# A sixth leading projection, earlier first weights and split norm steps in a two-layer diffusion trunk

## The chip, the cores and the metric

The kernel runs on one core of one Trainium2 chip. The core has five engines that work side by side: PE (matrix products; its weight loads are shown as PEld), DVE (vector operations), ACT (activations and copies), POOL (a slower general engine that here issues stores and computes powers) and SP (which here only issues loads). 16 DMA engines move data between the chip's main memory and the core. The metric is the time of one execution in microseconds (us). The time before is the median of 3 runs.

## The reference

A trunk of two layers handles two groups of tokens that share weights: 128 context tokens and 512 latent tokens, each a row of 2048 values in float32. Per layer:

```python
hp = rms_norm(xp, norm_g[layer]) * (1.0 + sc_p) + sh_p
hs = rms_norm(xs, norm_g[layer]) * (1.0 + sc_s) + sh_s
...
qa, ka, va, ga, ub, bb, cb, gb = split_cols(h @ w_in, EVEN_SPLIT)
...
y_a = merge_heads(o) * jax.nn.silu(ga)
y_b = gated_short_conv(ub, bb, cb, conv_w) * jax.nn.silu(gb)
return jnp.concatenate([y_a, y_b], axis=-1) @ w_out, new
```

Shift, scale and gate (`sh`, `sc`, `gt`) come from a conditioning product `silu(cond) @ ada_w + ada_b`, a weight matrix of 2048 x 6144 per layer with only two rows of input (one for the context tokens, one for the latent ones). `h @ w_in` is the input projection: in layer 0, 6656 columns for attention with a window (queries, keys, values, gate) and for a short gated convolution (u, b, c and its gate). Layer 1 has 6656 columns for two other kinds of attention. An output projection of 2048 x 2048 and a gated residual end each layer. The outputs are the new tokens and the keys and values of the context tokens.

## The kernel before, in words

**Layout.** Activations lie transposed: 128 features on the partitions, 640 tokens along a row (512 latent, then 128 context), so that a projection tile is 128 output columns x 640 tokens. Each of its two halves of 320 tokens is a PSUM buffer (`pa`, `pb`, or a half of `Sp`). Full float32 precision is had from three products of a high and a low part: `wh*hi`, `wh*lo`, `wl*hi` (lines 244 to 246). The inner dimension of 2048 is 16 chunks of 128, handled in four **quarters** of four chunks. The weights of a tile and quarter (256 KB) are loaded by SP (`load_raw`, line 225) into one of four `raw` buffers and split by ACT and DVE (`split`, lines 212 and 213) into four `wh` and four `wl` buffers.

**The leading stretch of layer 0.** `x_block` transposes and squares the input tokens. `ada_on_pe` (line 148) computes 512 columns of the conditioning product: it loads 2 MB pieces into two buffers by turns (line 155), multiplies them on PE (line 158, `T<-ada,sT`), copies (161), transposes (164) and adds up. Blocks 4 and 0 (scale and shift of the first four chunks) are computed first. Then `run_tiles` (line 277) takes the tiles of the input projection, called jobs. Its first few jobs **lead**: quarter after quarter, the normed rows `h` of that quarter are made (`h0_maker`, line 732), the conditioning blocks of the next quarter are loaded and multiplied (`ahead`, which is `ada_group`, line 715), and all leading jobs are multiplied by the quarter. The fourth quarter is cut in two. Some leading jobs are named in `TRANS`: they have no PSUM buffer of their own, but share buffer 0, are copied out after each quarter by ACT in the first (line 308) and added by DVE in the later ones (line 310), into a `sum` tile in a pool named `lead`. The others keep a PSUM buffer. Before, five jobs lead: u, k, v, q0 and q1 (the convolution's u, and keys, values and two query heads of the first pair of heads), and u, q0 and q1 are summed outside PSUM.

Of a quarter's leading weights, the first four are loaded before the rows are made, the others between the matmuls (line 302).

**After the lead.** Each later job is multiplied quarter by quarter. Between quarters a `slot` (line 269) advances the generators in `prep` (norms of queries and keys, lines 403 to 512), one step of `attn` (attention of a pair of heads, line 577), and `fill0`, which computes the remaining conditioning blocks on DVE (line 184). The leading jobs' own preparation is begun one by one there (`pending`). A gate job ends in `late_gate_job` (784): SiLU of the gate, then one multiplication of the finished attention output (line 799). `pair_then` (765) gets an empty dictionary in layer 0, so its outputs are copied (775); in layer 1 gates come first (`gate_job`, 1052), and the outputs are multiplied as they come (773). Small tiles named `stg` are in two buffers: a job's staged projection (`stage`, 379), the query norm's two tiles (451, 452) and the gate's (396, 793).

**End of a layer.** The last output tile is multiplied half by half (lines 354 to 370): the first half's four quarters, then `last(pp, 0)`, then the second half's, then `last(pp, 1)`. In layer 0, `out_last` (901) sums squares over the finished layer, takes the power -0.5 on POOL (919) and spreads it over the partitions by small matmuls (914, 922). In layer 1 `fin_last` (1113) adds the residual, transposes and stores.

The order in which an engine meets its instructions is fixed when the kernel is built: a planner goes by the order written and by a model of when operands and buffers are ready, and may put later matmuls ahead of earlier ones that wait. On the chip each engine then goes through its list in that order.

Of the kernel before, what the change touches and what calls it, by code (L numbers as in the profile page):

```python
# [11 lines left out]
F32 = mybir.dt.float32  # L12
# [8 lines left out]
P = 128  # L21
# [18 lines left out]

P_BUFS = 4
W_BUFS = 4
TRANS = [0, 3, 4]
GRACE = 3
RAW_AHEAD = 5
SPLIT_AHEAD = 3
# [8 lines left out]
def trunk_kernel(ctx: ExitStack, tc: tile.TileContext, I: dict, O: dict):  # L55
# [33 lines left out]
    vec = const.tile([P, 160], F32, name="vec")  # L89
    open_pool("start")  # L90
    sp = pre = pools["cur"]
    rows_a = pre.tile([P, P], F32, name="rows_a")
    nc.sync.dma_start(rows_a[0:16, :], I["c"].rearrange("b (k p) -> (b k) p", p=P))
    nc.scalar.dma_start(rows_a[16:32, :], I["c_ctx"].rearrange("(k p) -> k p", p=P))
    nc.scalar.dma_start(ident, I["k_ident"])
    nc.scalar.dma_start(rows_a[32:64, :], I["norm_g"].rearrange("l (k p) -> (l k) p", p=P))
    nc.scalar.dma_start(rows_a[64:112, :], I["ada_b"][0].rearrange("(k p) -> k p", p=P))
    rows_b = pre.tile([P, P], F32, name="rows_b")
    nc.scalar.dma_start(rows_b[0:48, :], I["ada_b"][1].rearrange("(k p) -> k p", p=P))
    nc.scalar.dma_start(rows_b[48:72, :], I["b_conv"][0].rearrange("t (k p) -> (t k) p", p=P))  # L100
    nc.scalar.dma_start(rows_b[72:74, :], I["c_out_norm"].rearrange("b (k p) -> (b k) p", p=P))
# [4 lines left out]
    ada_sb = pre.tile([P, 512], F32, name="ada_sb")  # L106
    h_t = [pre.tile([P, NT], F32, name=f"ht{i}") for i in range(2)]

    th = pre.tile([32, P], F32, name="th")
    A.activation(th, rows_a[0:32, :], AF.Tanh, scale=0.5)  # L110
    V.scalar_tensor_tensor(out=rows_a[0:32, :], in0=th, scalar=1.0, in1=rows_a[0:32, :],
                           op0=ALU.add, op1=ALU.mult)
# [116 lines left out]
    def split_w(raw):  # L229
        wh = wpool.tile(raw.shape, F32R, tag="wh", name="wh")  # L230
        wl = wpool.tile(raw.shape, F32R, tag="wl", name="wl")
        split(wh, wl, raw)
        return wh, wl
# [41 lines left out]
            credit[0] -= 1.0  # L275

    def run_tiles(jobs, w_ap, make_h, fill=None, rate=0.0, ahead=None, order=(0, 1, 2, 3), before=None,
                  last=None, by_half=False, trans=[], grace=0, cut=None):
        if trans:
            lp = tc.tile_pool(name="lead", bufs=1, side="right")  # L280
            lead_pool = lp.__enter__()
            sums = {n: lead_pool.tile([P, NT], F32, name=f"sum{n}") for n in trans}
            held = [n for n in range(2 + len(trans)) if n not in trans]

            leads = [n for m in range(len(held) + 1) for n in trans[m:m + 1] + held[m:m + 1]]
            leads += trans[len(held) + 1:]
        else:
            leads, held, lp = list(range(min(3, len(jobs)))), [], None
        lead = len(leads)
        pps = {n: (sums[n][:, 0:HALF], sums[n][:, HALF:NT]) if n in trans  # L290
               else new_pp(1 + held.index(n) if trans else n) for n in leads}
        units = [(pos, qd, js) for pos, qd in enumerate(order) for js in (cut if cut and pos == 3 else [(0, 4)])]
        for ui, (pos, qd, js) in enumerate(units):
            parts = {n: split_w(load_raw(w_ap, jobs[n][0], qd, js)) for n in leads[:W_BUFS]}
            for hv in [HV[:1], HV[1:]] if by_half and pos == 0 else [HV]:
                for k in range(4 * qd + js[0], 4 * qd + js[1]):
                    make_h(k, hv) if by_half else make_h(k)
                if ahead and ui + 1 < len(units):
                    ahead(*units[ui + 1][1:])
                for n in leads:  # L300
                    if n not in parts:
                        parts[n] = split_w(load_raw(w_ap, jobs[n][0], qd, js))
                    if n in trans:
                        pp = new_pp(0)
                        proj_q(pp, parts[n], qd, pos, alone=True, js=js)
                        for i, sl in HV:
                            if ui == 0:
                                A.copy(pps[n][i], pp[i][:, 0:HALF])
                            else:
                                V.tensor_add(pps[n][i], pps[n][i], pp[i][:, 0:HALF])  # L310
                    else:
                        proj_q(pps[n], parts[n], qd, pos, hv, js=js)
                    advance(attn, 1)

        quarters = [(col, qd) for col, _ in jobs[lead:] for qd in range(4)]
        raws, parts = {}, {}

        def run_ahead(t):
            for i in range(len(raws), min(t + RAW_AHEAD, len(quarters))):
                raws[i] = load_raw(w_ap, *quarters[i])  # L320
                j = len(parts)
                if j < t + SPLIT_AHEAD and j <= i:
                    parts[j] = split_w(raws[j])
            for j in range(len(parts), min(t + SPLIT_AHEAD, len(quarters))):
                parts[j] = split_w(raws[j])

        def begin(fn, pp):
            g = fn(pp)
            if g is not None:
                prep.append(g)  # L330
                advance(prep, 1)

        def settle():

            while pending:
                n = pending.pop(0)
                drain(prep)
                if before:
                    before(n)
                begin(jobs[n][1], pps[n])  # L340
            drain(prep)

        pending = list(range(lead))
        run_ahead(0)
        t = 0
        if before:
            settle()
        else:
            n = pending.pop(0)
            begin(jobs[n][1], pps[n])  # L350
        for i in range(lead, len(jobs)):
            fn = jobs[i][1]
            pp = new_pp((i - lead) % 2)
            split_last = last is not None and i == len(jobs) - 1
            for qd in range(4):
                proj_q(pp, parts[t], qd, qd, HV[:1] if split_last else HV)
                if before and qd == 0:
                    before(i)
                t += 1
                run_ahead(t)  # L360
                if pending and not prep:
                    n = pending.pop(0)
                    begin(jobs[n][1], pps[n])
                slot(fill, rate)
            if split_last:
                last(pp, 0)
                for qd in range(4):
                    proj_q(pp, parts[t - 4 + qd], qd, qd, HV[1:])
                last(pp, 1)
                return  # L370
            drain(prep)
            if i >= lead + grace and pending:
                settle()
            if lp and not pending and not prep:
                lp.__exit__(None, None, None)
                lp = None
            begin(fn, pp)
# [349 lines left out]
    ada_on_pe(0, 4)  # L727
    x_rows((0, 1, 2, 3))
    x_rows((4,))
    ada_on_pe(0, 0)  # L730

    def h0_maker(k):
        x = xT[k // 4][:, k % 4, :]
# [23 lines left out]
    def q_job(tag, gain, then=None):  # L757
        return lambda pp: q_gen(pools["cur"], pp, tag, gains[gain], then)

    def y_pair(i):  # L760
        t = pools["cur"].tile([P, 2, NT], F32, tag="y", name="y", bufs=2)
        y[i], y[i + 1] = t[:, 0, :], t[:, 1, :]
        return t

    def pair_then(width, kk, i, banded, gated):

# [74 lines left out]
    for i in range(4):  # L841
        kv, h = i // 2, 2 * i
        if i % 2 == 0:
            jobs.append((EV["k"] + kv * P, k_job("k0", I["cache_a_k"][0, 0, kv], "a_k_norm", O["new_a_k"][0, 0, kv])))
            jobs.append((EV["v"] + kv * P, v_job(I["cache_a_v"][0, 0, kv], O["new_a_v"][0, 0, kv])))
        jobs.append((EV["q"] + h * P, q_job("q0", "a_q_norm")))
        jobs.append((EV["q"] + (h + 1) * P, q_job("q1", "a_q_norm", pair_then(640, "k0", h, True, {}))))
        b_tiles(i)
        for j in (h, h + 1):
            jobs.append((EV["g"] + j * P, late_gate_job(j)))  # L850
    for i in range(4, 8):
        b_tiles(i)
    jobs.insert(0, jobs.pop(4))
    run_tiles(jobs, I["ev_w_in"][0], h0_maker, fill0, FILL0, ada_group, trans=TRANS, grace=GRACE, cut=((0, 2), (2, 4)))
    drain(prep)
    for _ in fill0:
        pass
# [43 lines left out]
    def out_last(pp, h):  # L901
        n, mp, sl = KT - 1, pools["cur"], HV[h][1]
        out_sum(n, pp, CS[:1] if h == 0 else CS[1:])
        if h == 0:
            st["sq"] = mp.tile([P, NT], F32, tag="sq", name="sq", bufs=1)
            st["rbc"] = mp.tile([P, NT], F32, name="rbc")
        A.activation(st["sq"][:, sl], x1[n][:, sl], AF.Square)
        starts = [HALF * h, HALF * h + P, HALF * (h + 1) - P]
        tot = psT()
        ss = small.tile([P, 3], F32, tag="ss", name="ss1")  # L910
        r = small.tile([P, 3], F32, tag="r", name="r1")
        for i, s in enumerate((st["acc"], st["sq"])):
# [4 lines left out]
            else:  # L917
                V.scalar_tensor_tensor(out=ss, in0=tot[:, 4:7], scalar=1.0 / D, in1=ss, op0=ALU.mult, op1=ALU.add)
        G.tensor_tensor(r, ss, half[:, 0:3], op=ALU.pow)
        rt = psT()  # L920
        for b, (o, w) in enumerate(((0, P), (P, P), (2 * P, HALF - 2 * P))):
            PE.matmul(rt[:, o:o + w], r[:, b:b + 1].to_broadcast([P, P]), ident[:, P - w:P], start=True, stop=True)
# [28 lines left out]
    def odd_start():  # L951
# [13 lines left out]
        st["con"] = con  # L965
        nc.sync.dma_start(con, I["c_out_norm"][0].partition_broadcast(P))
        V.tensor_scalar(con, con, 1.0 - LAM_INIT, None, ALU.mult)

    gated = {}

    def diff_then(h):
        def then():
# [76 lines left out]
                yield  # L1049
        save_y(2 * h, 2 * h + 1)  # L1050

    def gate_job(i):
        def f(pp):
            if i % 2 == 0:
                gated[i] = y_pair(i)
            gate(pools["cur"], pp, y[i])
        return f

    jobs = []
    heads = (3, 0, 1, 2)  # L1060
    for n, h in enumerate(heads):
# [51 lines left out]
    def fin_last(pp, h):  # L1113
# [3 lines left out]
            st["ot"] = fp.tile([P, 5, P], F32, tag="rp", name="ot", bufs=3)  # L1117
        xr, ot = st["xr", n], st["ot"]
        fin_sum(n, pp, CS[:1] if h == 0 else CS[1:])
        t = psT()  # L1120
        bs = (0, 1) if h == 0 else (2, 3, 4)
        for i, b in enumerate(bs):
# [59 lines left out]
```

## Time and profile before

| what | before |
|---|---|
| median of 3 runs | 2369.32 us (2366.55 to 2371.73) |
| the profiled execution | 2370.14 us |
| its span, first to last instruction | 2368.4 us |
| PE busy | 2320.9 us, 98% |
| DVE busy | 1368.7 us, 58% |
| ACT busy | 882.1 us, 37% |
| POOL busy | 126.2 us, 5% |
| moved by DMA | 304.08 MB, mean 128 GB/s |

How to read it: the span is cut into 40 equal slices of 59.2 us, and a digit is the busy share of an engine in a slice, in tenths (9 is 90% or more). A busy PE is not PE at its peak, since matmuls overlap; the distance between their starts tells the rate. "L158" is line 158 of the kernel. "a<-b" names what an instruction writes and reads. In a timeline row stand start, duration, engine, line, operation, and in brackets the idle time of the engine just before it with what ended that. SPq is the queue of loads that SP issues. The granted clock is the share of full speed that PE's throttle allowed.

### The profile page before, as it was taken

The numbers are of one execution on the slowest core, as the hardware profiler recorded it, in microseconds if no ns is written. First come the engines' busy times: TensorE is split into PE (matmuls) and PEld (weight loads), VectorE is DVE, ScalarE is ACT, GpSimd is POOL, SyncE is SP. The second block draws the span as 40 slices with busy tenths as digits, with TensorE's granted clock in tenths as the row PEclk, the third lists the DMA queues.
The fourth block names the chain that finished last, engine by engine and source line by source line (L and its number), as shares of the span: only waits on it lengthen the run. The fifth ranks groups of instructions, "written<-read, shape, count | busy, mean of one in ns | idle before, by whom it ended". The sixth has DMA issues, their size and how long they took to land.

```text
span 2368.4 us, 40878 instructions
## 1 busy us (share of the span) xinstructions
PE 2320.9 (98%) x16188; PEld 2246.1 (95%) x16188; DVE 1368.7 (58%) x2700; ACT 882.1 (37%) x1855; POOL 126.2 (5%) x173
## 2 busy tenths in 40 slices
PE   5989999999999999999999999999999999999999
PEld 3779999999999999999999999999999999999999
DVE  3468766765864555667865445354455554576662
ACT  4435442433422223222463443444334444453221
POOL 0000000000000000000010100001000000000000
PEclk8999999999999999999999999999999999999999
DMA  9983415424444445666431222212222212236552
GB/s 325 362 262 107 145 54 160 141 81 133 143 147 121 129 133 180 196 192 196 124 96 56 82 73 69 72 54 85 65 72 59 66 55 72 72 116 215 178 173 78
DMA packets 370045, 304.08 MB, mean 128 GB/s; under 512 B 16721, under 2 KB 310158, under 8 KB 369342
## 3 DMA queue, kind: packets, MB, share of 16 engines
q1 hardware_dynamic: 362448, 273.78, 38.1%
q0 software_dynamic: 6864, 27.47, 3.1%
q8 instruction: 127, 2.08, 0.4%
q14 instruction: 64, 0.52, 0.1%
q10 hardware_dynamic: 542, 0.22, 0.0%
HBM read 273.62 MB, written 27.79 MB: 127 GB/s over the span
## 4 chain that ended last, share of the span: by engine, by line
PE 91%; DMA 4%; DVE 2%; ACT 1%; issue 1%; POOL 0%; SPq 0%; ACTq 0%; DVEq 0%; POOLq 0%
PE pa L244 13%; PE pb L244 12%; PE pb L245 12%; PE pb L246 12%; PE pa L246 12%; PE pa L245 12%; PE T L538 2%; DMA ada<-in_ada_w 2%; PE S L550 1%; PE S L552 1%; PE S L551 1%; PE T L389 1%; PE T L599 1%; PE T L158 1%; DMA raw<-in_ev_w_in 1%
## 5 line engine op out<-in xcount | busy, mean ns | idle before, releaser
L212 ACT ACTIVATE wh<-raw 128x512 fp32r<-128x512 f32 (+1 forms) x549 | 343.6, 627 | 1045.4 <-PE pb L245 919.9
L213 DVE TENSOR_TENSOR wl<-raw,wh 128x512 fp32r<-128x512 f32 (+1 forms) x549 | 375.3, 684 | 556.3 <-ACT wh L212 506.4
L244 PE MATMUL pa<-h,wh 128*128 128x320 f32 x2112 | 669.7, 318 | 6.9 <-ACT h L212 4.9
L244 PE MATMUL pb<-h,wh 128*128 128x320 f32 x2112 | 654.6, 310 | 0.0
L245 PE MATMUL pa<-h,wh 128*128 128x320 f32 x2112 | 654.3, 310 | 0.0
L246 PE MATMUL pb<-h,wl 128*128 128x320 f32 x2112 | 654.1, 310 | 0.0
L246 PE MATMUL pa<-h,wl 128*128 128x320 f32 x2112 | 653.8, 310 | 0.0
L245 PE MATMUL pb<-h,wh 128*128 128x320 f32 x2112 | 653.8, 310 | 0.0
L244 PEld LDWEIGHTS pa<-h,wh 128*128 128x128 f32 x2112 | 397.2, 188 | 25.8 <-issue 16.5
L245 PEld LDWEIGHTS pa<-h,wh 128*128 128x128 f32 x2112 | 397.6, 188 | 3.2 <-issue 1.7
L246 PEld LDWEIGHTS pa<-h,wl 128*128 128x128 f32 x2112 | 396.9, 188 | 2.4 <-issue 2.4
L246 PEld LDWEIGHTS pb<-h,wl 128*128 128x128 f32 x2112 | 397.3, 188 | 1.3 <-issue 1.3
L244 PEld LDWEIGHTS pb<-h,wh 128*128 128x128 f32 x2112 | 397.6, 188 | 0.8 <-issue 0.8
L245 PEld LDWEIGHTS pb<-h,wh 128*128 128x128 f32 x2112 | 397.6, 188 | 0.0
L184 DVE SCALAR_TENSOR_TENSOR acc<-adaw,sT,acc 128x512 f32<-128x512 f32 x480 | 336.5, 746 | 22.9 <-DMA adaw<-in_ada_w 22.4
L524 ACT ACTIVATE p<-S,nm,rq 128x768 f32<-128x768 f32 (+3 forms) x120 | 101.3, 844 | 116.8 <-DVE nm L519 80.6
L517 DVE TENSOR_REDUCE nm<-S 128x1 f32<-128x768 f32 (+3 forms) x120 | 91.9, 766 | 23.3 <-PE S L552 22.8
L212 ACT ACTIVATE pth<-T 128x512 fp32r<-128x512 f32 (+1 forms) x132 | 65.8, 533 | 65.2 <-PE T L538 65.1
L213 DVE TENSOR_TENSOR ptl<-T,pth 128x512 fp32r<-128x512 f32 (+1 forms) x132 | 77.3, 608 | 6.4 <-ACT pth L212 5.1
L538 PE MATMUL T<-ident,p 128*128 128x128 f32 x452 | 64.4, 273 | 0.0
L458 ACT COPY qsw<-qx 32x512 f32<-32x512 f32 x96 | 59.3, 618 | 5.6 <-DVE m L434 4.2
L661 POOL DMA_DIRECT2D yd<-y x32 | 18.0, 561 | 752.3 <-DVE y L799 520.2
(248 smaller groups left out, 2300.1 us busy)
## 6 DMA issues: line engine op xcount, KB each, us to landing
adaw<-in_ada_w SPq DMA_DIRECT2D x256, 256.0 KB, 3.0
raw<-in_od_w_in SPq DMA_DIRECT2D x208, 256.0 KB, 2.8
raw<-in_ev_w_in SPq DMA_DIRECT2D x203, 256.0 KB, 2.9
ada<-in_ada_w SPq DMA_DIRECT2D x16, 2048.0 KB, 10.7
raw<-in_ev_w_out SPq DMA_DIRECT2D x64, 256.0 KB, 3.4
raw<-in_od_w_out SPq DMA_DIRECT2D x64, 256.0 KB, 2.8
yd<-y POOLq DMA_DIRECT2D x32, 320.0 KB, 3.0
yin<-yd SPq DMA_DIRECT2D x28, 320.0 KB, 4.8
```

Source lines behind the costliest of these rows:

```text
L158: PE.matmul(acc[32 * g:32 * g + 32, 0:wd], sT[:, kt, :], w[:, kt % m, :], start=(kt < 4), stop=(kt >= KT - 4), tile_position=(0, 32 * g))
L184: V.scalar_tensor_tensor(out=acc[c], in0=w, scalar=sT[:, kt, c:c + 1], in1=acc[c], op0=ALU.mult, op1=ALU.add)
L212: A.activation(hi, x, AF.Copy)
L213: V.tensor_sub(lo, x, hi)
L244: PE.matmul(ps, wh[:, i, :], hi[:, sl], start=(j == js[0] if alone else (pos == 0 and j == 0)), stop=False)
L245: PE.matmul(ps, wh[:, i, :], lo[:, sl], start=False, stop=False)
L246: PE.matmul(ps, wl[:, i, :], hi[:, sl], start=False, stop=(j == js[1] - 1 if alone else (pos == 3 and j == 3)))
L389: PE.transpose(t[:, i * P:(i + 1) * P], src(b), ident)
L458: A.copy(sw[32 * d:32 * d + 32, :], x[32 * (d ^ 1):32 * (d ^ 1) + 32, 0:NS])
L517: V.tensor_reduce(nm, s, axis=AX.X, op=ALU.max, negate=True)
L524: A.activation(p[:, 0:n], s, AF.Exp, scale=rsc, bias=nm, accum_out=l)
L538: PE.transpose(t[:, i * P:(i + 1) * P], p, ident)
```

## The change

- `TRANS` names a sixth leading job, and the order of the first ten jobs becomes u, k, v, g0, q0, q1, g1, c, b, h (before: u, k, v, q0, q1, c, b, h, g0, g1): the first head's gate leads, the second one's follows first. Six jobs lead, with four `sum` tiles.
- For the first pair of heads the gates are now handled by `gate_job`, and the attention's outputs are multiplied by the gate as they come.
- `ada_on_pe(0, 0)` is called by `run_tiles` (`lead_in`) after the first four weights have been loaded and split, and not before them.
- `out_last` and `fin_last` become generators. Their first part runs after the first half's quarters, and their later steps stand between the quarters of the second half. The last call, for the second half, runs without a break as before.
- The small start tiles `rows_a`, `rows_b` and `th` lie in the weight buffers `raw`, and the scratch memory for POOL's transfers is halved, to 8192 bytes a partition.

```diff
-TRANS = [0, 3, 4]
+TRANS = [0, 3, 4, 5]
...
-    rows_a = pre.tile([P, P], F32, name="rows_a")
+    rows_a = wpool.tile([P, P], F32, tag="raw", name="rows_a")
...
             parts = {n: split_w(load_raw(w_ap, jobs[n][0], qd, js)) for n in leads[:W_BUFS]}
+            if ui == 0 and lead_in:
+                lead_in()
...
             if split_last:
-                last(pp, 0)
+                first = last(pp, 0)
+                next(first)
                 for qd in range(4):
                     proj_q(pp, parts[t - 4 + qd], qd, qd, HV[1:])
-                last(pp, 1)
+                    next(first, None)
+                for _ in last(pp, 1):
+                    pass
                 return
...
-    ada_on_pe(0, 0)
...
+    def gate_job(i):
+        def f(pp):
+            if i - i % 2 not in gated:
+                gated[i - i % 2] = y_pair(i - i % 2)
+            gate(pools["cur"], pp, y[i])
+        return f
...
-        jobs.append((EV["q"] + (h + 1) * P, q_job("q1", "a_q_norm", pair_then(640, "k0", h, True, {}))))
+        jobs.append((EV["q"] + (h + 1) * P, q_job("q1", "a_q_norm", pair_then(640, "k0", h, True, gated))))
         b_tiles(i)
         for j in (h, h + 1):
-            jobs.append((EV["g"] + j * P, late_gate_job(j)))
+            jobs.append((EV["g"] + j * P, late_gate_job(j) if i else gate_job(j)))
...
-    jobs.insert(0, jobs.pop(4))
-    run_tiles(jobs, I["ev_w_in"][0], h0_maker, fill0, FILL0, ada_group, trans=TRANS, grace=GRACE, cut=((0, 2), (2, 4)))
+    u0, c0, b0, h0, g0, g1 = jobs[4:10]
+    jobs[0:10] = [u0, jobs[0], jobs[1], g0, jobs[2], jobs[3], g1, c0, b0, h0]
+    run_tiles(jobs, I["ev_w_in"][0], h0_maker, fill0, FILL0, ada_group, trans=TRANS, grace=GRACE, cut=((0, 2), (2, 4)),
+              lead_in=lambda: ada_on_pe(0, 0))
...
         A.activation(st["sq"][:, sl], x1[n][:, sl], AF.Square)
+        yield
...
         G.tensor_tensor(r, ss, half[:, 0:3], op=ALU.pow)
+        yield
         rt = psT()
...
         fin_sum(n, pp, CS[:1] if h == 0 else CS[1:])
+        yield
         t = psT()
...
-    nc = _bacc.Bacc("TRN2", target_bir_lowering=False, num_devices=1)
+    nc = _bacc.Bacc("TRN2", target_bir_lowering=False, num_devices=1, dynamic_dma_scratch_size=8192)
```

More of the change, by code (lines that the diff above doesn't have):

```diff
@@ L97, in trunk_kernel @@
     nc.scalar.dma_start(rows_a[64:112, :], I["ada_b"][0].rearrange("(k p) -> k p", p=P))
-    rows_b = pre.tile([P, P], F32, name="rows_b")
+    rows_b = wpool.tile([P, P], F32, tag="raw", name="rows_b")
     nc.scalar.dma_start(rows_b[0:48, :], I["ada_b"][1].rearrange("(k p) -> k p", p=P))
@@ L107, in trunk_kernel @@
     h_t = [pre.tile([P, NT], F32, name=f"ht{i}") for i in range(2)]
-    th = pre.tile([32, P], F32, name="th")
+    th = wpool.tile([32, P], F32, tag="raw", name="th")
     A.activation(th, rows_a[0:32, :], AF.Tanh, scale=0.5)
@@ L277, in run_tiles @@
     def run_tiles(jobs, w_ap, make_h, fill=None, rate=0.0, ahead=None, order=(0, 1, 2, 3), before=None,
-                  last=None, by_half=False, trans=[], grace=0, cut=None):
+                  last=None, by_half=False, trans=[], grace=0, cut=None, lead_in=None):
         if trans:
@@ L763, in y_pair @@
         return t
+    gated = {}
+    def gate_job(i):
[4 more added lines that the diff above has]
+        return f
     def pair_then(width, kk, i, banded, gated):
@@ L967, in odd_start @@
         V.tensor_scalar(con, con, 1.0 - LAM_INIT, None, ALU.mult)
-    gated = {}
     def diff_then(h):
@@ L1050, in diff_gen @@
         save_y(2 * h, 2 * h + 1)
[L1052 to L1057, printed above, removed]
+    gated.clear()
     jobs = []
```

## The prediction

> **What bounds the kernel now.** I read the page first, for the busy engine over the whole span, and then short windows of the start, where the page's slices show the only hole.
>
> ```profile
> span 2368.4 us, 40878 instructions
> ...
> PE   5989999999999999999999999999999999999999
> ...
> DMA  9983415424444445666431222212222212236552
> ...
> PE 91%; DMA 4%; DVE 2%; ACT 1%; issue 1%; POOL 0%; SPq 0%; ACTq 0%; DVEq 0%; POOLq 0%
> ```
>
> PE is full in every slice but the first three (180 us), and those are the slices in which the DMA engines are full. So an edit can pay in two ways only: it lets PE do useful work in the opening stretch, where PE sometimes waits for transfers, or it removes a later stall of PE. The profiled execution took 2370.14 us, 1.7 more than its span and 0.8 more than the median of 2369.32; I sum against this span.
>
> The windows view gives, per stretch, busy time and (count) for PE, PEld, DVE, ACT and POOL, then granted clock, DMA share and GB/s.
>
> ```profile
> 40.00:80.00 40.00, 33.38 (x224) 21.87 (x217) 15.05 (x31) 15.80 (x29) 0.00 (x0) 0.91 0.98 347
> 80.00:120.00 40.00, 37.81 (x281) 28.99 (x280) 22.22 (x47) 17.89 (x34) 1.25 (x2) 1.00 1.03 361
> ...
> 51.00:164.00 113.00, 104.06 (x763) 82.42 (x763) 55.17 (x125) 44.55 (x88) 2.31 (x4) 0.96 0.94 323
> 164.00:204.00 40.00, 38.06 (x267) 36.38 (x268) 37.82 (x75) 21.26 (x52) 6.46 (x5) 1.00 0.51 150
> 930.00:1010.00 80.00, 80.00 (x548) 80.00 (x547) 48.30 (x80) 20.82 (x32) 3.12 (x6) 1.00 0.65 205
> ```
>
> From 930 to 1010 almost nothing but projection matmuls runs: 80 us / 548 = **0.146 us** each at full clock. One projection tile is 16 chunks x 3 products x 2 halves = 96 of them, 14.0 us; a quarter of it is 24, 3.5 us. The leading stretch runs from 51 to 164 us: the first row below is its start, the second the first matmul after it, behind the last sum of a leading tile. In it DMA is 94% busy at 323 GB/s (361 while saturated) and PE 104 of 113 us: **both are nearly full**. That is why the sixth leading tile can't be free.
>
> ```profile
> 50.97 0.63 PE L244 MATMUL pa<-h,wh 128*128 128x320 f32 x1 [2.77 <-ACT h L212]
> ...
> 164.63 0.41 PE L244 MATMUL pa<-h,wh 128*128 128x320 f32 x1 [0.75 <-DVE sum L310]
> ```
>
> The waits view of PE for 50 to 164 us (total, times, longest), and the two matmul groups around the longest wait:
>
> ```profile
> PE T L158 <- DMA ada<-in_ada_w: 6.6, 2, 5.1
> PE pa L244 <- ACT h L212: 4.9, 3, 2.8
> ```
> ```profile
> 134.47 1.93 PE L158 MATMUL T<-ada,sT 128*32 128x256 f32 x32
> ...
> 142.67 3.56 PE L158 MATMUL T<-ada,sT 128*32 128x256 f32 x32 [5.12 <-DMA ada<-in_ada_w]
> ```
>
> The last conditioning transfer makes PE idle 5.1 us, and the same 32 matmuls then take 3.56 instead of 1.93 us: 1.6 us more, on a clock that has fallen. Another 1.5 us of transfer wait and 4.9 - 2.8 = 2.1 us of waits for the normed rows remain inside the stretch; the 2.8 stands before its start.
>
> **The change part by part.**
>
> *The sixth leading tile.* It takes 96 matmuls, 14.0 us, from after the stretch into it: -14.0 behind, +14.0 inside, less what fills idle time. When does PE reach the last conditioning matmuls? Three quarters with one more tile put 3 x 3.5 = 10.5 us in front of it, the later start (next edit) 1.5, and of the 3.6 us of smaller waits I take half as filled: 10.5 + 1.5 - 1.8 = 10.2. PE had been ready at 142.67 - 5.12 = 137.55, so now at 147.8. When does the transfer land? Up to there three and a half quarters of 256 KB more are loaded, 0.92 MB, at 361 GB/s 2.5 us: 145.2. So the 5.1 us wait and its 1.6 us of slow clock go, and what is late next is PE itself. Shift of the stretch's end: 14.0 + 1.5 - 1.8 - 6.7 = **+7.0**, against 14.0 us less behind it: **-7.0**. Bounds: if nothing is filled, 14.0 + 1.5 is paid and the edit costs 1.5; if only transfers bind, the last one lands 2.5 later and half a quarter of the sixth tile, 1.8, follows it, which gives +4.3 and -9.7.
>
> The tile's other work stands beside PE. Its sums cost ACT two copies in the first quarter and DVE two additions of 0.48 us in each later piece; its weight splits move from later.
>
> ```profile
> L310 DVE TENSOR_TENSOR sum<-sum,pa x12: 480/486/489, 89.7 to 164.1; 128x320 f32<-128x320 f32 x12
> ```
> ```profile
> 152.80:156.35 3.55, 3.55 (x27) 3.52 (x25) 2.56 (x10) 1.00 (x3) 0.00 (x0) 1.00 0.68 194
> ```
>
> DVE is busy 55 of the 113 us, so there is room. The last two leading tiles now share PSUM buffer 0 back to back; the second row is a place where two such tiles already adjoin (the end of one unit, the start of the next), and PE has no hole there. I take nothing.
>
> *First weights ahead of the second conditioning block.* SP's queue, and who waited on what it brought:
>
> ```profile
> 11.89 23.87 SPq L155 DMA_DIRECT2D ada<-in_ada_w  x4
> 35.81 5.65 SPq L225 DMA_DIRECT2D raw<-in_ev_w_in  x4
> 41.83 22.35 SPq L155 DMA_DIRECT2D ada<-in_ada_w  x4
> ```
> ```profile
> 43.53 1.92 PE L158 MATMUL T<-ada,sT 128*32 128x512 f32 x16 [1.78 <-DMA ada<-in_ada_w]
> 47.54 0.66 PE L164 MATMUL T<-ident,ada_sb 128*128 128x128 f32 x4 [2.08 <-ACT ada_sb L161]
> ```
> ```profile
> 44.16 2.85 ACT L212 ACTIVATE wh<-raw 128x512 fp32r<-128x512 f32 x4 [4.52 <-DMA raw<-in_ev_w_in]
> 46.92 0.57 ACT L161 COPY ada_sb<-T 128x512 f32<-128x512 f32 x1
> ```
>
> Gained: the four splits (2.85 us of ACT) no longer stand between the block's matmuls (done at 45.45) and its copy (46.92), 1.4 us. Lost: the DMA engines are full (0.98 from 40 us on), so 1 MB of weights put in front delays the block's last transfer by 1.05 MB / 361 GB/s = 2.9 us. Net **+1.5** on the first projection matmul (already in the sum above). [...]
>
> *The gate in the attention.* The first pair's five outputs are multiplied by the gate on DVE (0.418 us each) in place of copies on ACT, and two multiplications of 0.823 us go.
>
> ```profile
> L773 DVE TENSOR_TENSOR y<-T,y x20: 414/418/425, 1823.4 to 2123.0; 128x256 f32<-128x256 f32 x20
> ```
> ```profile
> L799 DVE TENSOR_TENSOR y<-y,gg x18: 816/823/827, 222.1 to 2127.3; 128x640 f32<-128x640 f32 x18
> ```
>
> That is 2.1 - 1.6 = 0.4 us more on DVE, 1.8 less on ACT, with PE full from 204 us on: nothing on the path. But the first convolution tile is now consumed a tile later, and until then the staged u keeps one of two staging buffers, of which the first query norm needs both. The query's preparation therefore starts a tile later, in a stretch where DVE is 95% busy (164 to 204). PE's waits there, from the view for 164 to 1140 us:
>
> ```profile
> PE T L389 <- DVE m L434: 1.3, 1, 1.3
> ...
> PE pa L244 <- DVE sum L310: 0.7, 1, 0.7
> ```
>
> Bounds: these 2.0 us could go or double; I take 0. The cover is the projections of the following tiles.
>
> *Moved start rows and the halved DMA scratch.* Three small tiles use the weight buffers before the first weights need them, the last free after the transposes near 10 us, ahead of the first weight issue: 0. The scratch serves POOL's transfers; no row shows POOL held by it, and POOL is busy 126 of 2368 us, so I take 0. If it did hold POOL back by one landing (3.0 us in the page's list of issues), later stores would cover it.
>
> *Norm steps between quarters.* At the end of the first output projection:
>
> ```profile
> 1150.22 0.54 DVE L883 SCALAR_TENSOR_TENSOR x<-pa,hgt,o 128x320 f32<-128x320 f32 x1
> ...
> 1151.38 0.83 PE L914 MATMUL T<-ones,sq 128*128 128x1 f32 x6 [1.07 <-ACT sq L907]
> ...
> 1152.49 1.25 POOL L919 TENSOR_TENSOR r<-ss,half 128x3 f32<-128x3 f32 x1 [8.48 <-DVE ss L918]
> ...
> 1153.80 1.54 PE L922 MATMUL T<-ident,r 128*128 128x128 f32 x6 [1.04 <-POOL r L919]
> ```
> ```profile
> 1153.80:1159.80 6.00, 6.00 (x24) 6.00 (x25) 3.04 (x6) 2.88 (x6) 0.00 (x0) 0.50 0.15 44
> 1159.80:1165.80 6.00, 6.00 (x45) 6.00 (x45) 3.40 (x9) 3.11 (x7) 0.97 (x2) 1.00 0.47 147
> ```
>
> Two stalls of 1.07 and 1.04 us, and then 6 us at half clock: 24 instructions where the next 6 us hold 45, so some 6 x (1 - 24/45) = 2.8 us lost. Ceiling 4.9. A quarter of one half is 12 matmuls, 1.8 us. From the last small matmul (1152.2) to the power's result (1153.7) is 1.5 us, so one quarter covers the second stall. The first depends on DVE, which wrote x only at 1150.22; no more matmuls stand in front of it than now, and I keep it. Whether the clock then still falls is open: between 1.0 and 4.9 I take **-2.5**. [...] The last step at the end of layer 1 is split too, but its only wait is for the second half, which stays where it was:
>
> ```profile
> PE T L1123 <- DVE xr L1096: 0.6, 1, 0.6
> ```
>
> **Sum:** -7.0 - 2.5 = -9.5: span 2358.9, own time 2360.6, against the median 0.8 less: **2360 us**.
>
> **The rivals.** About 0.2% (4.7 us) is what a measurement of this kernel can tell from no change.
>
> *Full already.* PE fills none of the small or large waits, because its order is fixed at build and the added matmuls may not fall where the waits are: lead +1.5 and norm -2.5 give 2368. For it: PE idled 5.1 us at 137.55 although projections of the same quarter were ready behind. Against: the added work lies ahead of that point by count. With part of the wait filled it lies between, down to 2365. Chance 0.20.
>
> *SP's queue as the new bound, slower.* Behind the conditioning loads SP now issues two late weights, not one, and the next quarter's fourth weight then needs a buffer that the second leading tile frees, not the first: 3.5 us of PE later at a full quarter's border, with the next conditioning loads behind it. SP's waits for 50 to 164 us show the place:
>
> ```profile
> SPq L155 <- PE T L158: 26.0, 5, 6.7
> SPq L225 <- DVE wl L213: 16.4, 9, 4.5
> ```
>
> If DMA then stands idle that long at each border (3 x 3.5 + 1.8 = 12.3 us), the last transfer lands at 145.2 + 12.3 = 157.5 and the lead ends 4.3 + 12.3 = 16.6 later, 2.6 over the 14.0; PE idles at each, and a falling clock costs some 2 us a time, as after 1153.8: +8 more, norm -2.5: 2377. It decides from about 2.5 us of idle DMA at a border, where the 9.5 are used up. Against it: two loads of 2 MB are under way at once, 11.6 us of transfer. Chance 0.12.
>
> *Transfers alone bind,* all waits filled and the clock kept: -9.7 - 4.9 = -14.6: 2355. Chance 0.13. My forecast, 2356 to 2364.5: 0.55.
>
> **The numbers.** Faster by over 0.2% is the forecast and the last rival, 0.68; within 0.2% the first rival, 0.20; slower 0.12. The range goes from 2354 (transfers alone) to 2372 (the first rival with the stretch after the lead 2 us worse and some of the queue's idle), which leaves some 0.15 out.
>
> **What would show it.** The lead's end at 171.6 instead of 164.6 us; no wait of 5 us for the last conditioning transfer; the first projection matmul at 52.5; at the norm one stall instead of two, and fewer than 6 us at clock 0.5. Wrong would be: PE waits of over 9 us inside the lead, DMA share well under 0.94 there, or PE holes between 170 and 260 us.

## The result and the profile after

The changed kernel takes **2358.76 us** (median of 5, 2357.41 to 2364.68) against 2369.32 (of 5 runs too, 2366.55 to 2371.73): ratio **0.9961**, 95% interval 0.9945 to 0.9976. That is 9.2 us less by the ratio and 10.6 by the two medians. Run again later beside other kernels it took 2361.31 against 2371.78: 0.9953 (0.9940 to 0.9967). The forecast was 2360. The profiled execution of the changed kernel took 2359.88 us. From its page:

```profile
span 2358.1 us, 40886 instructions
...
PE   5999999999999999999999999999999999999999
...
DMA  9984425425444445666431222212222212236652
```

The third slice of PE is full now, and the DMA slices are nearly those of before. Two windows, the leading stretch and its part up to the last conditioning matmuls (columns as before):

```profile
56.60:172.70 116.10, 111.92 (x846) 94.41 (x843) 61.44 (x140) 46.23 (x93) 2.31 (x4) 1.00 0.94 314
56.60:146.20 89.60, 87.89 (x670) 72.32 (x667) 41.65 (x89) 35.95 (x69) 2.31 (x4) 1.00 1.02 348
```

PE is busy 112 of 116 us where it was 104 of 113, at a clock of 1.00 where it was 0.96, beside an equally full DMA. Most of that difference in the clock is a matter of where the stretch begins. In the kernel before, the half clock of the start reaches 6 us into it:

```profile
51.00:57.20 6.20, 6.20 (x25) 2.93 (x25) 5.01 (x8) 4.45 (x8) 0.00 (x0) 0.50 0.87 322
```

In the changed kernel that half clock ends at 56.9 us, as the first projection matmul starts (56.64). PE's waits from 50 to 172 us, and the matmuls around its start, the last conditioning transfer and its end:

```profile
PE T L158 <- DMA ada<-in_ada_w: 2.8, 2, 1.6
PE pa L244 <- DVE sum L312: 1.1, 2, 0.8
PE pb L244 <- DVE sum L312: 0.8, 1, 0.8
PE T L164 <- ACT ada_sb L161: 0.8, 1, 0.8
PE T L164 <- DVE red L166: 0.6, 1, 0.6
```
```profile
53.26 3.45 PE L158 MATMUL T<-ada,sT 128*32 128x512 f32 x16 [1.21 <-DMA ada<-in_ada_w]
56.64 0.54 PE L244 MATMUL pa<-h,wh 128*128 128x320 f32 x1
```
```profile
146.21 1.93 PE L158 MATMUL T<-ada,sT 128*32 128x256 f32 x32 [1.59 <-DMA ada<-in_ada_w]
```
```profile
172.75 0.39 PE L244 MATMUL pa<-h,wh 128*128 128x320 f32 x1
```

The wait of 5.12 us for the last conditioning transfer is 1.59, and its 32 matmuls run at full clock (1.93 us instead of 3.56). A second execution of the same kernel, after_again below, was less lucky there:

```profile
146.47 3.64 PE L158 MATMUL T<-ada,sT 128*32 128x256 f32 x32 [2.64 <-DMA ada<-in_ada_w]
```

The stretch ends at 172.75 instead of 164.63, 8.1 later, with 14.0 us more work in it. It begins later too: the plan puts the next block's 16 matmuls (53.26) ahead of the first projection matmul.

To see where two traces part, I number the projection matmuls (lines 244 to 246, 13,056 in each kernel, 96 a tile) and subtract the start times of equal numbers. Changed minus before: -9.1 us behind six tiles, -6.4 behind 26, -6.2 behind 47, -7.5 behind 52 (the first of the output projection), -7.6 at number 6450 and -10.6 at number 6600 (before and after the norm), -10.3 at the last. So there are three steps: the leading stretch (-6.2), one at the end of layer 0's input tiles (-1.3) and one at the norm (-3.0). The rest of the kernel is the same to 0.3 us.

The second step answers to this wait of before. In the changed kernel PE waits for nothing between 800 and 1100 us:

```profile
926.42 0.41 PE L244 MATMUL pa<-h,wh 128*128 128x320 f32 x1 [1.18 <-DVE gg L797]
```

At the norm of the changed kernel:

```profile
1141.36 0.55 DVE L899 SCALAR_TENSOR_TENSOR x<-pa,hgt,o 128x320 f32<-128x320 f32 x1
...
1143.44 0.80 PE L931 MATMUL T<-ones,sq 128*128 128x1 f32 x6
...
1145.89 0.88 PE L940 MATMUL T<-ident,r 128*128 128x128 f32 x6 [0.52 <-POOL r L936]
...
1154.27 0.88 PE L940 MATMUL T<-ident,r 128*128 128x128 f32 x6 [0.70 <-POOL r L936]
```
```profile
1145.90:1151.90 6.00, 5.59 (x40) 5.32 (x40) 4.84 (x12) 3.85 (x9) 0.26 (x1) 1.00 0.42 123
1151.90:1157.90 6.00, 5.30 (x41) 4.56 (x42) 4.04 (x15) 3.88 (x12) 1.38 (x2) 1.00 0.33 109
```

The first stall is gone, the second is half, one of 0.70 has come in the second half's chain, and the clock stays at 1.00. How long the first stall is goes with how soon DVE, which is at conditioning work, writes `x` after the last matmul of the first half: 1.1 us after it here, with no stall, and 2.3 in the kernel before, with one of 1.07.

### The profile page after: what moved, and what is told of

It reads as the page before. It is cut to its first block, busy times and chain, and to the rows that moved or that the text cites. A ratio compares the mean times of both kernels' runs of the same rounds, so it can differ in the third digit from the quotient of the medians.

```text
span 2358.1 us, 40886 instructions
## 1 busy us (share of the span) xinstructions
PE 2317.2 (98%) x16188; PEld 2242.1 (95%) x16188; DVE 1371.5 (58%) x2712; ACT 880.8 (37%) x1853; POOL 126.5 (5%) x173
## 4 chain that ended last, share of the span: by engine, by line
PE 93%; DMA 2%; DVE 1%; ACT 1%; issue 1%; SPq 1%; POOL 0%; ACTq 0%; DVEq 0%; POOLq 0%
PE pa L244 13%; PE pb L244 13%; PE pb L245 13%; PE pb L246 13%; PE pa L245 13%; PE pa L246 13%; PE T L543 2%; DMA ada<-in_ada_w 2%; PE S L555 1%; PE S L557 1%; PE S L556 1%; PE T L394 1%; PE T L158 1%; PE T L604 1%; PE T L605 1%
## 5 line engine op out<-in xcount | busy, mean ns | idle before, releaser
L213 DVE TENSOR_TENSOR wl<-raw,wh 128x512 fp32r<-128x512 f32 (+1 forms) x550 | 375.7, 684 | 556.8 <-ACT wh L212 514.2
L213 DVE TENSOR_TENSOR ptl<-T,pth 128x512 fp32r<-128x512 f32 (+1 forms) x132 | 77.3, 609 | 5.4 <-ACT pth L212 4.1
```

The costliest lines, as they stand in the source:

```text
L213: V.tensor_sub(lo, x, hi)
```

## The experiments

Twelve kernels ran in three groups of four, each group on one chip beside the kernel before, to which "ratio" refers. The last three columns are from one profiled execution each, in us: the end of the leading stretch (first projection matmul behind it), the start of the next projection matmul behind 24 tiles, and the time from number 6450 to 6600 of the projection matmuls, where the norm lies (150 x 0.146 = 21.9 without it).

| kernel | leads | time | ratio (95%) | lead's end | 24 tiles | norm |
|---|---|---|---|---|---|---|
| before (first measurement) | 5 | 2369.32 | 1 | 164.6 | 497.6 | 32.7 |
| changed (first measurement) | 6 | 2358.76 | 0.9961 (0.9945 to 0.9976) | 172.8 | 491.4 | 29.6 |
| after_again | 6 | 2361.31 | 0.9953 (0.9940 to 0.9967) | 173.0 | 491.6 | 29.7 |
| lead_alone | 6 | 2359.85 | 0.9948 (0.9935 to 0.9960) | 170.2 | 488.8 | 33.6 |
| weights_after | 6 | 2360.55 | 0.9953 (0.9941 to 0.9964) | 171.6 | 490.1 | 34.1 |
| no_norm | 6 | 2361.36 | 0.9957 (0.9944 to 0.9971) | 172.5 | 491.1 | 34.4 |
| c_leads | 6 | 2365.05 | 0.9973 (0.9962 to 0.9985) | 172.2 | 493.4 | 31.6 |
| seven_leads | 7 | 2366.68 | 0.9977 (0.9966 to 0.9988) | 189.3 | 493.1 | 32.3 |
| five_leads | 5 | 2367.75 | 0.9981 (0.9973 to 0.9990) | 160.8 | 493.6 | 29.0 |
| weights_alone | 5 | 2369.72 | 0.9987 (0.9978 to 0.9996) | 164.2 | 497.2 | 33.5 |
| norm_only | 5 | 2369.71 | 0.9991 (0.9982 to 0.9999) | 167.6 | 500.2 | 31.2 |
| gate_alone | 5 | 2371.47 | 0.9999 (0.9990 to 1.0008) | 164.2 | 497.3 | 29.6 |
| parity | 5 | 2372.44 | 1.0002 (0.9992 to 1.0012) | 166.2 | 499.5 | 33.6 |
| four_leads | 4 | 2378.63 | 1.0037 (1.0025 to 1.0049) | 154.5 | 504.8 | 29.3 |

The kernel before took 2372.15, 2371.73 and 2371.78 in the three groups, 2.4 to 2.8 above the first measurement, so the times in the expectations below would stand about 2.5 higher there. A ratio of 0.001 is 2.4 us. The profiled executions of five_leads (2361.40), gate_alone (2366.55) and four_leads (2372.98) lie 5 to 6 us below the medians of these kernels, so their last three columns don't stand for a typical execution.

**One edit alone, or taken back.** norm_only is the kernel before with the split norm steps; no_norm is the changed kernel without them:

```diff
...
                 for qd in range(4):
                     proj_q(pp, parts[t - 4 + qd], qd, qd, HV[1:])
+                    next(first, None)
...
```

> The kernel before with the split norm steps alone. Theory (three separate sources: lead -6.2 us, PSUM buffer at the end of layer 0's input projection -1.4, norm -2.75): 2369.3 - 2.75 = 2366.6; the clock stays at full speed around the norm, and all of the difference arises between 1115 and 1175 us. Rival (the norm's stalls went because the rest of the schedule shifted): no change, 2369.3, and half a clock after the norm as before.

> The changed kernel with the norm steps undivided, as before. Theory: 2358.8 + 2.75 = 2361.5, with 6 us of half clock back after the norm. Rival (norm steps are worth nothing by themselves): 2358.8.

norm_only came out 2.1 us (0.2 to 4.3) lower, which fits the theory's 2.75. But no_norm lies at 0.9957 beside 0.9953 and 0.9961 for the changed kernel: taking the split back cost nothing that can be told. And the clock doesn't go with the edit. Two windows rows, gate_alone without the split and weights_after with it, and the waits of gate_alone from 1138 to 1165 us:

```profile
1152.00:1158.00 6.00, 5.14 (x36) 5.14 (x37) 3.28 (x8) 3.60 (x9) 0.81 (x1) 1.00 0.17 49
```
```profile
1152.00:1158.00 6.00, 5.01 (x28) 3.81 (x29) 3.22 (x9) 2.77 (x9) 1.64 (x2) 0.67 0.38 125
```
```profile
PE T L935 <- POOL r L932: 1.0, 1, 1.0
PE T L927 <- ACT sq L920: 0.7, 1, 0.7
```

gate_alone has both stalls and keeps a clock of 1.00; weights_after, steps split, is granted 0.67. The norm column says the same: 29.3 to 34.4 us without the split (seven executions, mean 32.4), 29.0 to 34.1 with it (seven, mean 31.1). Most of the spread of 5 us is the clock's: by the traces' records of the granted clock, 0 to 10.2 us of this stretch are at half clock, and at least some in five of seven executions without the split and in four of seven with it. A difference of 1.3 us between the means can't be told from nothing beside that spread.

The traces also hold a reason why the split could bring something on five leads and nothing on six. PE's waits from 1125 to 1175 us, first of norm_only, then of no_norm:

```profile
PE T L918 <- ACT sq L910: 1.5, 1, 1.5
PE T L927 <- POOL r L923: 0.7, 1, 0.7
```
```profile
PE T L927 <- ACT sq L920: 1.1, 1, 1.1
PE T L935 <- POOL r L932: 0.5, 1, 0.5
```

The waits for `r` in these rows belong to the second half, and the one of the first half (1.04 us before) is gone in both, with the split and without it. In the kernel before, 3 projection matmuls stand between the sums of squares and the matmuls that need `r`. The split makes that 9 on five leads. On six leads the plan has 8 there already, and the split makes it 7. The first stall stays in norm_only (1.5 us, with DVE writing `x` 3.2 us late), so the split alone does not take it away.

weights_after takes back the earlier weights, weights_alone makes them the only edit:

```diff
             parts = {n: split_w(load_raw(w_ap, jobs[n][0], qd, js)) for n in leads[:W_BUFS]}
+            if ui == 0 and lead_in:
+                lead_in()
```

> The changed kernel with the second conditioning block loaded ahead of the first weights again. Theory (the full DMA queue makes the block late when weights go first): the first projection matmul comes some 2 us earlier than in the changed kernel, and the time is 0.7 to 2 us lower, 2357 to 2358. Rival (loading weights first gains, since the splits no longer stand in the block's way): 1 to 2 us higher, 2360 to 2361.

> The kernel before with the first weights loaded ahead of the second conditioning block alone. Theory (full DMA queue): 0.7 to 2 us above before. Rival (the splits out of the block's way, weights there early, another order planned from it): 2 to 4 us below before, which would account for what five leads with all other edits gained.

With six leads the times can't be told apart (0.9953 and 0.9953). In the traces the changed kernel (twice) and no_norm, with the earlier weights, end their lead at 172.5 to 173.0 and the two without at 170.2 and 171.6. That fits the theory's sign, but 1 to 2.8 us is no more than single executions of one program differ by there (last section). SP's queue in the changed kernel shows the order, and ACT's the late block:

```profile
11.76 5.57 SPq L155 DMA_DIRECT2D ada<-in_ada_w  x2
17.38 12.52 SPq L225 DMA_DIRECT2D raw<-in_ev_w_in  x4
30.00 33.70 SPq L155 DMA_DIRECT2D ada<-in_ada_w  x6
```
```profile
50.76 0.58 ACT L161 COPY ada_sb<-T 128x512 f32<-128x512 f32 x1 [10.98 <-PE T L158]
```

The block's copy stands at 50.76 instead of 46.92. With five leads weights_alone was 3.1 us (0.9 to 5.2) faster, against the theory and as the rival had it, though its lead ends where that of gate_alone does (164.2) and its one trace lies 0.4 us from before throughout. What it gained is not shown.

gate_alone has the new place of the gate, and lead_alone the sixth leading tile with it. Both also have the moved start rows and the halved scratch, though the expectation of gate_alone says "no other edit":

```diff
-    jobs[0:10] = [u0, jobs[0], jobs[1], g0, jobs[2], jobs[3], g1, c0, b0, h0]
+    jobs[0:10] = [u0, jobs[0], jobs[1], jobs[2], jobs[3], g0, g1, c0, b0, h0]
```

(this for gate_alone, with `TRANS = [0, 3, 4]`, both without the split and without the earlier weights)

> Five leading tiles as before, with the first pair's gates next after the lead and applied in the attention; no other edit. Theory (nothing on PE's path): within 1.5 us of before. Rival (five leads with all other edits lay 4.4 us below before since the gate's early place pays): 3 to 5 us below before.

> The sixth leading tile alone (with the gate in the attention that it needs): the norm steps undivided and the second conditioning block ahead of the first weights, as before. Theory: 6.2 + 1.4 = 7.6 us below before, and within 2 us of the changed kernel, 2362 to 2365. Rival (the three edits only pay together): at most 4 us below before.

> The changed kernel itself, beside the three below on the same chip, since single executions have turned out to differ by 2 to 3 us in the leading stretch and by up to 5 us around the norm. Theory: 9 to 11 us below the kernel before on this chip, 2361 to 2363; the leading stretch again ends 7 to 10 us later than in the kernel before, and the half clock after the norm comes or stays away by chance.

The gate's new place, the moved rows and the scratch together are worth nothing (0.9999), as expected. **So the sixth leading tile, without the split and the earlier weights, gives 12.3 us (9.5 to 15.4), all that the whole change gives.** Its waits in the lead, and its first matmul:

```profile
PE T L158 <- DMA ada<-in_ada_w: 2.9, 2, 1.5
PE pa L244 <- ACT h L212: 2.8, 1, 2.8
PE pa L244 <- DVE sum L312: 1.0, 2, 0.8
PE pb L244 <- DVE sum L312: 0.5, 1, 0.5
```
```profile
50.66 0.64 PE L244 MATMUL pa<-h,wh 128*128 128x320 f32 x1 [2.77 <-ACT h L212]
```

The start is that of before (50.97), its 2.8 us wait stands ahead of it, and the end comes 5.6 us later at 170.2. Behind 24 tiles it is 8.8 us ahead of before, and at its last projection matmul 9.5, the lower end of that interval.

**How many tiles may lead.** four_leads lets the second query head follow (with the convolution's c between), five_leads is the changed kernel with the first gate behind the lead, seven_leads adds the second gate:

```diff
-TRANS = [0, 3, 4, 5]
+TRANS = [0, 3, 4, 5, 6]
```

> The kernel before with four leading tiles (the second query head follows the lead, after the convolution's c). Theory (idle PE in the lead is what a leading tile fills, and transfers set the end when there is more idle than work): 14.0 us go behind the lead, whose end comes only some 4 to 6 us sooner; the last tile then uses the other PSUM buffer, -1.4: 2376 to 2378. Rival (PE bounds the lead, tiles can be moved for nothing): within 1.5 us of before, 2368 to 2371.

> The changed kernel with five leading tiles (the first head's gate follows the lead, but is still applied in the attention; norm steps split, weights first). Theory: the sixth lead's 6.2 us and the free PSUM buffer's 1.4 us come back: 2366.4. Rival (the gate in the attention or the earlier weights carry the gain): at most 2 us above the changed kernel, 2359 to 2361.

> The changed kernel with a seventh leading tile, the second head's gate. Theory: only 6.1 us of PE waits are left in the changed kernel's lead, of which a third to a half can be filled: -2 to -3; the last tile uses the PSUM buffer of before again, +1.4: 2357 to 2359. Rival (each leading tile gives the same 6 us): 2354. Second rival (late weights of the lead hold up the conditioning loads): over 2362.

four_leads is 8.8 us (5.9 to 11.6) slower than before, about as expected, though its lead ends 10.1 us sooner and not 4 to 6. five_leads is 4.5 (2.4 to 6.4) faster, which fits 2.9 and excludes the rival. Its lead ends 3.4 us or more sooner than those of the other kernels with five: PE's longest wait there for a conditioning transfer is 1.9 us, and 4.6 to 6.2 in the other five-lead kernels. Why the last transfer came in time in that one execution is open. Set beside the changed kernel (0.9961 and 0.9953), five_leads gives the sixth tile a worth of 5 to 7 us, not 12.3. The edits don't add up: those beside the tile give 4.5 us on five leads and nothing that can be told on six.

seven_leads missed: 5.5 us faster than before instead of 10 or more, as the second rival had it. Its lead ends 16.6 us after that of the changed kernel, with 14.0 us of work more. Its windows up to the last conditioning matmul, two of SP's waits in its lead, those for weight buffers, and then the same two of the changed kernel:

```profile
57.10:163.80 106.70, 102.68 (x770) 86.19 (x770) 46.20 (x100) 37.91 (x73) 2.32 (x4) 0.97 0.90 303
```
```profile
SPq L225 <- DVE wl L213: 22.7, 13, 3.6
SPq L225 <- DVE sum L312: 14.4, 8, 3.6
```
```profile
SPq L225 <- DVE wl L213: 13.9, 9, 2.9
...
SPq L225 <- DVE sum L312: 6.4, 5, 1.9
```

DMA moves 303 GB/s where the changed kernel has 348, and SP stands 17 us longer before weight loads whose buffers aren't free, with the conditioning loads behind them. That is the place that the forecast's slower rival names, one tile later than it was set. But PE idles little more for it: its waits from 50 us to the lead's end come to 6.7 us, against 6.1 in the changed kernel. What is new is half clock behind two of them, of 2.0 us each:

```profile
128.70:132.10 3.40, 3.40 (x27) 2.24 (x19) 0.00 (x0) 0.37 (x1) 0.00 (x0) 0.50 1.06 349
152.60:156.00 3.40, 3.40 (x14) 3.40 (x14) 0.60 (x3) 0.38 (x1) 0.00 (x0) 0.50 0.13 39
```

These 6.8 us at a granted 0.50 cost 3.4 (an estimate, half of them), and the lead is 16.6 - 14.0 = 2.6 us worse than the tile's work. So in this trace the seventh tile finds nothing left to fill. That the standing queue makes the loss is not shown. The opposite end, PE's waits in the lead of four_leads:

```profile
PE pa L244 <- ACT h L212: 10.1, 3, 3.7
```

There PE has nothing to do before the next quarter's rows, and DMA is 99% busy:

```profile
51.70:154.50 102.80, 93.45 (x664) 70.17 (x665) 47.07 (x109) 40.72 (x79) 2.32 (x4) 0.91 0.99 339
```

**Another sixth tile.** c_leads lets the convolution's c lead instead of the gate, which is applied late as before:

```diff
+    jobs[0:11] = [u0, c0, jobs[0], jobs[1], jobs[2], jobs[3], b0, h0, jobs[10], g0, g1]
```

> The changed kernel with another sixth leading tile: the convolution's c in place of the first head's gate, with the gate applied after the attention as before. Theory (what leads does not matter): as the changed kernel within 1.5 us, 2357.3 to 2360.3. Rival (the gate in the attention, or its being ready early, carries the gain): 2362 or more.

It is 6.4 us (3.6 to 9.0) faster than before, not 10, which is the rival's figure, although gate_alone gives the gate itself nothing. The lead ends at the same place (172.2); some 2 us are lost by the end of 24 tiles and the rest later, half clock at the norm included. So what leads may matter by 3 to 5 us, though the intervals of c_leads and the changed kernel overlap; which wait takes them was not separated.

**The buffer at the end of layer 0's input tiles.** parity gives the output projection's first tile the other PSUM buffer:

```diff
-               else new_pp(1 + held.index(n) if trans else n) for n in leads}
+               else new_pp(1 + held.index(n) if trans else (1, 0, 2)[n] if before else n) for n in leads}
```

> The kernel before with one edit: the first tile of the output projections takes PSUM buffer 1 and the second buffer 0, so that the first doesn't wait for the buffer that the last input tile's gate still reads. Theory (the wait of 1.2 us at 925 us is that buffer): that wait goes, all of the difference arises there, -1.3: 2368.0. Rival (the wait went in the changed kernel since its DVE had less to do by then): no change before 925 us and the wait stays.

In its trace the difference to before falls from +1.95 us to +0.61 behind 52 tiles: -1.34, what the changed kernel gains there. Some tiles later it gives 0.8 of it back. Of its waits from 800 to 1100 us this one is left, and it isn't the gate's:

```profile
PE pb L244 <- DVE x L883: 0.5, 1, 0.5
```

The 0.8 goes at that wait, at 972 us, and the changed kernel doesn't have it. Jobs behind the lead take buffers 0 and 1 by turns; with six leads the last one uses buffer 1, and the output projection begins with 0. The five kernels with five leads and the old order of buffers wait 0.5 to 1.2 us for `gg` there, those with four and six don't. With seven the buffer is that of before again, and the expected 1.4 us still didn't come back, since the plan has small conditioning matmuls in that place. The whole run can't show 1.3 us (ratio 1.0002).

## Why the prediction was right

- **Where the time could come from.** Right: PE full and DMA full in the lead, and the tile's 14.0 us partly into idle time.
- **The sixth tile.** The terms were 14.0 of work, 8.5 of it into waits and slow clock, and 1.5 for a later start. lead_alone tests the first two by themselves: forecast +5.5 for the lead's end, measured 170.21 - 164.63 = +5.6. The sum was better than its parts. PE's waits between the first projection matmul and the lead's end fell from 9.6 to 4.5 us, by 5.1 where 6.9 were forecast. The rest is half clock, 9.7 us before and 3.5 in lead_alone, worth 3.1 where 1.6 were forecast: the 6 us at half clock from the start of the stretch are in no term of the prediction, and that they were fewer here is luck. With the earlier weights +7.0 was forecast, and +8.1 and +8.4 measured. The last conditioning matmuls were to be reached at 147.8 with the transfer landed at 145.2; PE was there at 144.6 and the transfer at 146.2, so the transfer was still the later one, by 1.59 us, and not PE, as the working had it. The clock stayed full, as forecast, but in after_again, with 2.64 us of that wait, it did not.
- **The earlier weights.** Forecast +1.5. In the lead with six tiles the traces have that sign, within what executions differ by, and the first projection matmul came later than forecast (56.64, not 52.5), 3.4 us of it a block of matmuls that the plan moved ahead of it. For the whole kernel it made no difference that can be told.
- **The stretch behind the lead, the gate, the moved rows.** Forecast nothing. gate_alone, which has the gate's new place, the moved rows and the scratch, gives nothing (0.9999); the changed kernel's lead gives 14.0 - 8.1 = 5.9, and 6.2 stand behind 47 tiles. None of these three was tried by itself.
- **Missed:** the 1.3 us at 926 us. The wait stands in the view of waits of before; that the count of leads decides which PSUM buffer the last tile holds I did not see.
- **The norm, the step that failed.** Its -2.5 was matched by the -3.0 of the first trace, and still it was not right. The stall that I kept went in the changed kernel (in norm_only it stayed, at 1.5 us), one came in the second half, and the bulk of both numbers is a half clock (6.8 us of it in the trace of before, none in that of the changed kernel) that comes and goes with and without the split. And the working took the second stall as it stood with five leads, behind 3 projection matmuls: the sixth tile's plan has 8 there without any split. On six leads the split is worth nothing that these runs can tell (no_norm 0.9957, changed 0.9961 and 0.9953).

So the sum came out because the lead's term held in its total (about -8.5 without the earlier weights) and because, in the first trace, a clock that stayed full at the norm and an unseen -1.3 filled what the split did not bring. That part is luck.

## What to carry to other kernels

Where PE and DMA are both nearly full, put down for each the waits that are left and their ends: work moved in costs its length less the waits and the half clock that it takes away (here the sixth tile's 14.0 us moved the lead's end by 5.6 to 8.4), and when those are used up a further tile costs more than it brings (here the seventh, 16.6 us for 14.0). A matching total, or one trace in which a step has the forecast size, does not show that the step caused it; take each edit back by itself and try it alone, since the worths needn't add up, and compare equal instructions of two traces to find where they part. After any change in the number of tiles, ask which buffer the last of them holds.

## What the runs showed of the hardware

- The length of a stall alone doesn't tell whether the granted clock falls. Two waits of about 1 us with six one-column matmuls between were followed by 6 us at 0.50 in the kernel before, and by 1.00 in gate_alone (0.7 and 1.0 us). A wait of 1.59 us in the changed kernel's lead left it at 1.00, and one of 0.9 us in weights_after, before six one-column matmuls, did not (0.82 from 1140 to 1146 us, where it lies, and 0.90 in the next 6 us). The 150 projection matmuls at the norm took 29.0 to 34.4 us over the 14 profiled executions, mostly by this.
- In the clock records of the traces of before and of the changed kernel the granted clock is 1.00 or 0.50, and it changes only on a grid of 3.41 us, to within 0.02 us. In the kernel before it falls and rises at 142.60 and 146.01 (one step of the grid), and at 1152.95 and 1159.77 (two); in the changed kernel it does so at 53.51 and 56.92 (one). Counted back to the start of the span, the grid passes at 2.66 us in the one trace and at 2.31 in the other, so equal stalls can fall differently into it. That this is what decides was not tried.
- before, parity and norm_only run the same program up to 800 us. Their leads end at 164.6, 166.2 and 167.6 us, and behind 24 tiles they stand at 497.6, 499.5 and 500.2: differences of 2 to 3 us in the lead need more than one trace.
- PE kept to the order of its list: in the kernel before it stood idle from 137.55 to 142.67 us for a conditioning transfer, though the seven projection matmuls that follow in the same tile (from 146.16) had their rows and weights by 135.4, when DVE's last split before the wait ended (L213, from 134.99).
- Projection matmuls of 0.31 us start 0.146 us apart (before, 930 to 1010 us), so they overlap. POOL's power over 128x3 took 1.06 us on average in the kernel before (L919), DVE's 128x3 instructions ahead of it 0.15 and 0.16 (L916, L918).
